# S5 outputs that read the scan's states directly: state tables with chunks innermost, and another order of the stage

## The chip, the cores and the metric

The kernel runs on one core of a Trainium2 chip. A core has a matmul engine (TensorE, "PE" in the profile, with its weight loads as "PEld"), a vector engine (VectorE, "DVE"), an activation engine (ScalarE, "ACT"), GpSimd ("POOL") and a queue for transfers (SyncE, "SP"); they share an on-chip memory of 128 partitions (SBUF) and accumulators that TensorE writes (PSUM). The metric is the device time of one execution in microseconds, as the median of the runs.

## The reference

An input of 256 frames by 2048 features runs through two layers, all in float32. The first layer's mixer, the one that the change touches, is a diagonal state-space layer (S5): 128 groups of 16 features, each with 64 complex states.

```python
u = h @ w_in                                    # 256 x 2048
u_g = u.reshape(bsz, seq, S5_GROUPS, S5_GROUP)  # 128 groups of 16
bu = einsum('blgc,gpc->blgp', u_g, bb)          # complex, 64 states each
s  = associative_scan(s_t = ab * s_(t-1) + bu_t) over the frames
y  = einsum('blgp,gcp->blgc', s_re, c_re) - einsum('blgp,gcp->blgc', s_im, c_im)
z  = gelu(y + d_skip * u)
z  = z * sigmoid(z @ w_glu)
return z @ w_out
```

After it come a squared-ReLU MLP, then a chunked gMLP mixer and a second MLP, with RMS norms around each. These take the most time and the change leaves them as they are.

## The kernel before

The program is written in the order in which it runs: every engine works through its own queue in program order, and no scheduler moves anything. An instruction that waits holds up all that stands behind it on its engine.

**Large products.** A weight is taken in panels. One step of a panel (`kstep`) takes a 128-row slice of a weight, splits it into a high part (ScalarE, L145) and a low part (VectorE, L146), and issues 12 matmuls of 128x512 (L171). The left side is a slab, which `tgroup` fills from transposes (L271) with a high part (L275, ScalarE) and a low part (L276, VectorE). `w_in` alone is multiplied without the split: `win_panel(p, hooks)` runs panel p in 16 steps of two 128x512 matmuls (L183), and after step n calls what stands in `hooks[n]`.

**The S5 stage.** The 256 frames form 64 chunks k of 4 frames j. The 128 groups form two halves h of 64 groups, handled in pairs: 32 rows r per half, with two groups gp = 0, 1 in each row; i = 0, 1 is the real or imaginary part. The states of a group fill 64 partitions.
- `u_tr`, `u_load`: u is transposed and, through DRAM (`ud`), laid out by groups.
- `v_group(h, b)`: for eight rows r, matmuls (L830) give what each chunk adds to the states, in an accumulator; four copies of 64x512 (ScalarE L841, VectorE L839) put it into `s_t`.
- `scan(i)`: a scan over the 64 chunks in five levels up and five down. A level is four VectorE operations (L859 to L862): two products with a table `sc_t` into temporaries, two additions into the states. It handles 31, 15, 7, 3 or 1 chunks of 32 floats each: 992, 480, 224, 96 or 32 elements a partition. Scans 0 and 1 belong to h = 0 (16 rows each), 2 and 3 to h = 1. `scan_some(i, n)` issues the next n levels.
- `y_states(h, b)`: copies the states of eight rows from `s_t` into `sst` (ScalarE L884, VectorE L882), shifted by one chunk, with real and imaginary parts stacked on 128 partitions.
- `y_group(h, b)`: for each of eight rows, two matmuls on 128 partitions (L895: states times the table that `prep_w2` made in `xw`) and two on 64 (L898: u times `t_t`), then eight gelu activations (L904) into `zv`.
- `z_t(h, b)` is `tgroup` of `zv` into the slab for GLU. `idle_fill(n)` issues n matmuls without use (L264).

The trace records a plain float32 matmul as two entries ("passes" below), so a `win_panel` step is L183 x4 in it and a row of y_group L895 x4 and L898 x4.

Accumulators come from a pool of three; panel 2 of `w_in` holds one while v and y groups share the rest, and the GLU panel `pg` later holds two. `s_t` lies with chunks outermost and rows innermost:

```python
    s_t = [g6.rearrange("p (k i r) -> p k i r", i=2, r=32)] + [
        t.rearrange("p (k i r) -> p k i r", i=2, r=16) for t in (g3[:, 0:2048], g0[:, 0:2048])]
```

Loads of weights and `u_load` are issued on the SP queue in program order.

Of the kernel before, what the change touches and what calls it, by code (L numbers as in the profile page):

```python
# [30 lines left out]
def kernel(  # L31
# [672 lines left out]
    def table_mul(dst, tab0, h, st_sw, j, tm):  # L704
# [15 lines left out]
          for s in (g4[:, 0:2048], spare, g5[:, 0:2048], g0[:, 2048:4096])]  # L720
    t_t = [s[:, 2048:4096].rearrange("p (r j c) -> p r j c", j=4, c=16) for s in (g4, g5)]

    s_t = [g6.rearrange("p (k i r) -> p k i r", i=2, r=32)] + [
        t.rearrange("p (k i r) -> p k i r", i=2, r=16) for t in (g3[:, 0:2048], g0[:, 0:2048])]
    ust = [g6[:, 0:2048].rearrange("p (n d) -> p n d", n=2)] + [
        g7[:, 0:1024].rearrange("p (n d) -> p n d", n=2)] * 2
    utp = [g6[:, 2048:4096].rearrange("p (b a t) -> p b a t", b=4, a=2)] + [
        g7[:, 1024:2048].rearrange("p (b a t) -> p b a t", b=2, a=2)] * 2
    sst = [g8[:, i * 1024:(i + 1) * 1024].rearrange("p (r q k) -> p r q k", q=2, k=64)
           for i in range(2)]  # L730

# [4 lines left out]
    def prep_w2(h, j):  # L736
        table_mul(x_t[h], 8 + 2 * j, h, bc_t[h, "c"], j, tmw)

# [82 lines left out]
    def u_zero(q):  # L821
        G.memset(ub[q], 0.0)

    def u_of(h, r):
        return ub[2 * h + r // 16][:, r % 16, :]

    def v_group(h, b):
        ps = accp.tile([128, 1024], F32, tag="acc", name="acc")
        for q in range(8):
            T.matmul(ps[:, q * 128:(q + 1) * 128], lhsT=w1_t[h, b][:, q, :],  # L830
                     rhs=u_of(h, 8 * b + q), start=True, stop=True)
        sv, r0 = sv_of(h, b)
        pv = ps.rearrange("p (r g k) -> p g r k", g=2, k=64)
        for gp in range(2):
            for ri in range(2):
                o = sv[gp * 64:gp * 64 + 64, :, ri, r0:r0 + 8].rearrange("p k r -> p r k")
                i = pv[ri * 64:ri * 64 + 64, gp]
                if gp and h == 0:
                    V.tensor_copy(o, i)  # L839
                else:  # L840
                    S.activation(out=o, in_=i, func=AF.Copy)  # L841

    def sv_of(h, b):
        return (s_t[0], 8 * b) if h == 0 else (s_t[1 + b // 2], 8 * (b % 2))

    def scan(i, tmp):

        h, r0, nr = i // 2, 16 * (i % 2), 16
        s = s_t[0][:, :, :, r0:r0 + 16] if h == 0 else s_t[i - 1]

        def level(lv, k0):
            d, step = 1 << lv, 2 << lv
            n = (62 - k0) // step + 1
            dst = s[:, k0:k0 + (n - 1) * step + 1:step]
            src = s[:, k0 - d:k0 - d + (n - 1) * step + 1:step]
            t = [x[:, 0:n * 2 * nr].rearrange("p (n i r) -> p n i r", i=2, r=nr) for x in tmp]
            a, b = [sc_t[:, lv, k, h, :, r0:r0 + nr].unsqueeze(1).to_broadcast([128, n, 2, nr])
                    for k in (0, 1)]
            V.tensor_tensor(out=t[0], in0=src, in1=a, op=ALU.mult)  # L859
            V.tensor_tensor(out=t[1][:, :, ::-1, :], in0=src, in1=b, op=ALU.mult)  # L860
            V.tensor_tensor(out=dst, in0=dst, in1=t[0], op=ALU.add)
            V.tensor_tensor(out=dst, in0=dst, in1=t[1], op=ALU.add)  # L862
# [10 lines left out]

    def y_states(h, b):
        dst = sst[b % 2]
        sv, r0 = sv_of(h, b)
        for ri in range(2):
            for gp in range(2):
                o = dst[ri * 64:ri * 64 + 64, :, gp, 1:64]
                i = sv[gp * 64:gp * 64 + 64, 0:63, ri, r0:r0 + 8].rearrange("p k r -> p r k")  # L880
                if gp and h:
                    V.tensor_copy(o, i)  # L882
                else:
                    S.activation(out=o, in_=i, func=AF.Copy)  # L884

    def y_group(h, b):
        dst = sst[b % 2]
        w2 = xw[h].rearrange("p (g m) -> p g m", m=64)
        tv = t_t[h].rearrange("p r j c -> p r (j c)")
        ps = accp.tile([128, 1024], F32, tag="acc", name="acc")  # L890
        for q in range(8):
            r = 8 * b + q
            o = [ps[0:64, gp * 512 + q * 64:gp * 512 + q * 64 + 64] for gp in range(2)]
            for gp in range(2):
                T.matmul(o[gp], lhsT=dst[:, q, gp, :], rhs=w2[:, 2 * r + gp, :], start=True,  # L895
                         stop=False)
            for gp in range(2):
                T.matmul(o[gp], lhsT=u_of(h, r)[gp * 64:gp * 64 + 64, gp * 64:gp * 64 + 64],  # L898
                         rhs=tv[gp * 64:gp * 64 + 64, r, :], start=False, stop=True)
        c0 = b * 256  # L900
# [12 lines left out]
    with tc.manual_schedule():  # L913
# [71 lines left out]
        def c(f, *args):  # L985
            return lambda: f(*args)
# [28 lines left out]
        def scan_some(i, n):  # L1015
            for _ in range(n):
                next(scs[i], None)

        def sst_zero():
            for t in sst:  # L1020
                G.memset(t[:, :, :, 0:1], 0.0)

        ps = win_panel(1, {
# [11 lines left out]
        ps = win_panel(2, {  # L1035
            0: [c(u_tr, 1, b) for b in range(2)] + [c(u_load, 2), c(y_states, 0, 0)],
            4: [c(y_states, 0, 1)],
            6: [c(v_group, 1, 0)],
            7: [c(v_group, 1, 1), c(scan_some, 2, 99)],
            8: [c(idle_fill, 7), c(y_group, 0, 0)],  # L1040
            10: [c(y_group, 0, 1), c(y_states, 0, 2)],
            12: [c(y_states, 0, 3)],
        })
        u_out(2, ps, r0[0])
        idle_fill(4)
        for b in range(2):
            u_tr(2, b)
        u_zero(3)
        u_load(3)
        y_group(0, 2)  # L1050
        issue_cast(glu_p[0][0] + 2, True)
        slab_z.append(Slab("g6"))
        z_t(0, 0)
        y_group(0, 3)
        more_raw()
        z_t(0, 1)
        pg = new_acc()
        state["hold"] = False
        run_panel(glu_p[0], slab_z, pg, 0, 1)
        z_t(0, 2)  # L1060
        v_group(1, 2)
        z_t(0, 3)
        run_panel(glu_p[0], slab_z, pg, 1, 2)
        v_group(1, 3)
        y_states(1, 0)
        y_states(1, 1)
        slab_z.append(Slab("g3"))
        run_panel(glu_p[0], slab_z, pg, 2, 3)
        scan_some(3, 99)
        idle_fill(4)  # L1070
        y_group(1, 0)
        run_panel(glu_p[0], slab_z, pg, 3, 5)
        y_group(1, 1)
        z_t(1, 0)
        run_panel(glu_p[0], slab_z, pg, 5, 8)
        z_t(1, 1)
        y_states(1, 2)
        y_states(1, 3)
        idle_fill(4)
        run_panel(glu_p[0], slab_z, pg, 8, 9)  # L1080
        y_group(1, 2)
        run_panel(glu_p[0], slab_z, pg, 9, 10)
# [245 lines left out]
```

## Time and profile before

| | |
|---|---|
| runs | 2737.99, 2736.59, 2735.10 us; median 2736.59 |
| profiled execution | 2737.9 us, its span 2735.9 us |
| granted TensorE clock, mean | 0.994 |
| busy share of the span | PE 98%, PEld 79%, DVE 58%, ACT 46%, POOL 0% |
| chain that ended last, by engine | PE 91%, DVE 3%, ACT 2% |
| chain, by line | L171 84%, L183 2%, L830 1% |
| S5 stage, from the first state matmul to GLU step 10 | about 120 to 285 us of the span |

The share of busy time belongs to the whole span, of which the S5 stage is a small part; within it one has to look at stretches (busy time of each engine between two moments), at the chain of work that ended last in order of time, and at single waits. Times in rows of the trace count from the start of the span.

### The profile page before, as it was taken

The page shows a single profiled execution, that of the slowest core. Times are in us where ns is not written, and L with a number is a line of the kernel's source. Part 1 is how long each engine was busy: PE and PEld are TensorE (multiplying, and loading weights), DVE is VectorE, ACT ScalarE, POOL GpSimd, SP SyncE. Part 2 cuts the span into 40 slices and gives each one's busy share as a digit, 9 for nine tenths or more (in the row PEclk, how much of TensorE's full clock was granted, in tenths as well). Part 3 has the DMA queues.
Part 4 walks back from the last instruction along what each step waited for, and adds up shares of the span by engine and source line. Part 5 has one row for each costly group of instructions (what it writes and reads, how often), then busy time and mean ns, then how long its engine had stood idle before and what let it go on. Part 6 is the DMA issues. An engine that isn't in the chain of part 4 may idle for free.

```text
span 2735.9 us, 30661 instructions
## 1 busy us (share of the span) xinstructions
PE 2680.0 (98%) x12395; PEld 2153.3 (79%) x12395; DVE 1591.8 (58%) x1831; ACT 1258.4 (46%) x1438; POOL 12.8 (0%) x23
## 2 busy tenths in 40 slices
PE   8998999999999999999999999999999999999997
PEld 4556887888888888778887788888878888888885
DVE  6686456545555555575558645555575455555555
ACT  5465545444443444454444544444454444443443
POOL 0100000000000000000000000000000000000000
PEclk9999999999999999999999999999999999999998
DMA  7432475555555555655556555555655555555553
GB/s 188 149 112 93 159 238 169 189 185 191 192 185 193 192 184 186 199 201 187 197 191 209 185 189 193 188 185 198 231 173 183 199 185 187 191 191 187 194 189 108
DMA packets 149629, 502.30 MB, mean 184 GB/s; under 512 B 21856, under 2 KB 30192, under 8 KB 148208
## 3 DMA queue, kind: packets, MB, share of 16 engines
q1 hardware_dynamic: 148896, 500.02, 54.3%
q8 instruction: 97, 1.59, 0.2%
q10 hardware_dynamic: 592, 0.33, 0.0%
q14 instruction: 44, 0.36, 0.0%
HBM read 494.02 MB, written 6.29 MB: 183 GB/s over the span
## 4 chain that ended last, share of the span: by engine, by line
PE 91%; DVE 3%; ACT 2%; issue 1%; DMA 0%; SPq 0%; DVEq 0%; ACTq 0%
PE acc L171 84%; PE acc L183 2%; PE tr L271 2%; PE tr L1241 1%; DVE lo L146 1%; PE acc L830 1%; PE tr L264 0%; ACT g L884 0%; PE acc L895 0%; DVE g L328 0%; PE acc L898 0%; ACT g L841 0%; DVE g L352 0%; DVE g L347 0%; ACT big L904 0%
## 5 line engine op out<-in xcount | busy, mean ns | idle before, releaser
L171 PE MATMUL acc<-hi,sl_g 128*128 128x512 f32 x6912 | 1881.7, 392 | 2.6 <-DVE g L328 1.1
L171 PEld LDWEIGHTS acc<-hi,sl_g 128*128 128x128 f32 x6912 | 1294.3, 188 | 276.9 <-DVE g L328 2.4
L146 DVE TENSOR_TENSOR lo<-raw,hi 128x1024 fp32r<-128x1024 f32 x652 | 797.2, 1225 | 689.4 <-ACT hi L145 682.2
L171 PE MATMUL acc<-lo,sl_g 128*128 128x512 f32 x3456 | 1067.9, 390 | 11.3 <-DVE lo L146 11.3
L145 ACT ACTIVATE hi<-raw 128x1024 fp32r<-128x1024 f32 x652 | 691.0, 1061 | 805.9 <-PE acc L171 805.7
L171 PEld LDWEIGHTS acc<-lo,sl_g 128*128 128x128 f32 x3456 | 649.5, 188 | 147.9 <-DVE lo L146 12.1
L146 DVE TENSOR_TENSOR lo<-spare,hi 128x1024 fp32r<-128x1024 f32 x212 | 259.5, 1225 | 287.1 <-ACT hi L145 287.1
L145 ACT ACTIVATE hi<-spare 128x1024 fp32r<-128x1024 f32 x212 | 224.8, 1062 | 323.7 <-PE acc L171 323.7
L183 PE MATMUL acc<-raw,g 128*128 128x512 f32 x256 | 117.5, 604 | 0.1
L276 DVE TENSOR_TENSOR sl_g<-tr,sl_g 128x512 fp32r<-128x512 f32 x104 | 67.3, 686 | 64.5 <-ACT sl_g L275 64.5
L275 ACT ACTIVATE sl_g<-tr 128x512 fp32r<-128x512 f32 x104 | 57.1, 595 | 86.9 <-PE tr L271 86.5
L183 PEld LDWEIGHTS acc<-raw,g 128*128 128x128 f32 x256 | 47.1, 193 | 50.2 <-issue 49.3
L1148 DVE TENSOR_TENSOR g<-acc,g 128x1024 f32<-128x1024 f32 x48 | 56.4, 1217 | 0.0
L271 PE MATMUL tr<-ident,big 128*128 128x128 f32 x416 | 55.0, 273 | 0.1
L271 PEld LDWEIGHTS tr<-ident,big 128*128 128x128 f32 x416 | 48.3, 141 | 8.3 <-ACT big L1242 1.7
L1127 DVE TENSOR_TENSOR big<-big 128x1024 f32<-128x1024 f32 x32 | 39.2, 1226 | 5.2 <-ACT big L1126 3.0
L1126 ACT ACTIVATE big<-acc,st 128x1024 f32<-128x1024 f32 x32 | 35.8, 1119 | 8.7 <-PE acc L171 8.7
L264 PE MATMUL tr<-ident 128*128 128x512 f32 x68 | 33.2, 625 | 6.6 <-DVE sl_g L314 6.6
L1242 ACT ACTIVATE big<-tr,bsT 128x384 f32<-128x384 f32 x32 | 18.6, 582 | 41.6 <-PE tr L1241 40.6
L904 ACT ACTIVATE big<-acc 32x256 f32<-32x256 f32 x64 | 23.9, 374 | 27.4 <-PE acc L898 26.7
L1234 DVE TENSOR_TENSOR big<-big,g 128x768 f32<-128x768 f32 x32 | 30.7, 958 | 1.1
L841 ACT ACTIVATE g<-acc 64x512 f32<-64x512 f32 x24 | 25.7, 1069 | 11.4 <-PE acc L830 11.1
(172 smaller groups left out, 850.5 us busy)
## 6 DMA issues: line engine op xcount, KB each, us to landing
raw<-in_ffn_w_up_dram SPq DMA_DIRECT2D x96, 1024.0 KB, 5.1
raw<-in_ffn_w_down_dram SPq DMA_DIRECT2D x96, 1024.0 KB, 5.2
raw<-in_sgu_w_in_dram SPq DMA_DIRECT2D x72, 1024.0 KB, 5.1
raw<-in_sgu_w_out_dram SPq DMA_DIRECT2D x36, 1024.0 KB, 5.3
spare<-in_ffn_w_up_dram SPq DMA_DIRECT2D x32, 1024.0 KB, 5.0
spare<-in_ffn_w_down_dram SPq DMA_DIRECT2D x32, 1024.0 KB, 5.3
spare<-in_sgu_w_in_dram SPq DMA_DIRECT2D x24, 1024.0 KB, 5.0
raw<-in_s_w_in_dram SPq DMA_DIRECT2D x15, 1024.0 KB, 6.3
```

What stands on the lines that cost most here:

```text
L145: S.activation(out=hi, in_=src, func=AF.Copy)
L146: V.tensor_tensor(out=lo, in0=src, in1=hi.bitcast(F32), op=ALU.subtract)
L171: T.matmul(half(ps, j), lhsT=l, rhs=r[:, j * 512:(j + 1) * 512], start=first and w == 0, stop=last and w == which[-1])
L183: T.matmul(ps[n][:, j * 512:(j + 1) * 512], lhsT=lhs[n], rhs=raw_t[i][:, k, j * 512:(j + 1) * 512], start=first, stop=last)
L264: T.matmul(ps, lhsT=ident, rhs=ident.unsqueeze(1).to_broadcast([128, 4, 128]), start=True, stop=True)
L271: T.transpose(out=ps[:, a * 256 + n * 128:a * 256 + n * 128 + 128], in_=src(kt + a, n), identity=ident)
L275: S.activation(out=slab.hi[:, o:o + 512], in_=ps, func=AF.Copy)
L276: V.tensor_tensor(out=slab.lo[:, o:o + 512], in0=ps, in1=slab.hi32[:, o:o + 512], op=ALU.subtract)
L1126: S.activation(out=tmp[n], in_=ps[n], func=AF.Relu, scale=rs[:, n:n + 1])
L1127: V.tensor_tensor(out=tmp[n], in0=tmp[n], in1=tmp[n], op=ALU.mult)
L1148: V.tensor_tensor(out=acc[:, n, c], in0=ps[n], in1=acc[:, n, c], op=ALU.add)
L1234: V.tensor_tensor(out=vt[:, :, c], in0=vt[:, :, c], in1=t[h % 2].unsqueeze(1).to_broadcast([128, 2, HD]), op=op)
```

## The change

It lays the states out as `(i r k)`, chunks innermost and shifted by one chunk, so that chunk 0 is zero (`s_zero`, on GpSimd, L854) and y_group reads `s_t` as it stands. The table of `prep_w2` is laid out by real and imaginary part on the 64 partitions of each group (`w2_t`), by four half-sized additions in place of one (L741, L746). `y_states`, `sst` and `sst_zero` go. y_group issues per row two matmuls with u (L896) and four with states (L899), all on 64 partitions, in pairs for the two halves of the rows. v_group writes 64x8x63, contiguous in k (L849 VectorE, now for h = 1; L851 ScalarE). The scan's operations (L872 to L875) step through k, which is innermost. The fillers (7, 4, 4 and 4) go, and the calls from panel 2 on stand in another order: scan 3 goes level by level between GLU steps.

```diff
-    s_t = [g6.rearrange("p (k i r) -> p k i r", i=2, r=32)] + [
-        t.rearrange("p (k i r) -> p k i r", i=2, r=16) for t in (g3[:, 0:2048], g0[:, 0:2048])]
+
+    s_t = [g6.rearrange("p (i r k) -> p i r k", i=2, r=32)] + [
+        t.rearrange("p (i r k) -> p i r k", i=2, r=16) for t in (g3[:, 0:2048], g0[:, 0:2048])]
...
-    sst = [g8[:, i * 1024:(i + 1) * 1024].rearrange("p (r q k) -> p r q k", q=2, k=64)
-           for i in range(2)]
+    w2_t = [s.rearrange("p (r i j c) -> p r i j c", i=2, j=4, c=16) for s in xw]
 
     def prep_w2(h, j):
-        table_mul(x_t[h], 8 + 2 * j, h, bc_t[h, "c"], j, tmw)
+
+        (a, b), (tm1, tm2) = bc_t[h, "c"], tmw
+        gs = slice(64 * h, 64 * h + 64)
+        for o, i, k in ((tm1, a, 0), (tm2, b, 1)):
+            V.tensor_tensor(out=o, in0=i, op=ALU.mult,
+                            in1=tabB[:, 8 + 2 * j + k, gs].unsqueeze(2).to_broadcast([128, 64, 16]))
+        for ri in range(2):
+            for gp in range(2):
+                q = slice(ri * 64, ri * 64 + 64)
+                V.tensor_tensor(out=w2_t[h][gp * 64:gp * 64 + 64, :, ri, j, :],
+                                in0=tm1[q, gp::2, :], in1=tm2[q, gp::2, :], op=ALU.add)
 
...
     def v_group(h, b):
...
         pv = ps.rearrange("p (r g k) -> p g r k", g=2, k=64)
         for gp in range(2):
             for ri in range(2):
-                o = sv[gp * 64:gp * 64 + 64, :, ri, r0:r0 + 8].rearrange("p k r -> p r k")
-                i = pv[ri * 64:ri * 64 + 64, gp]
-                if gp and h == 0:
+                o = sv[gp * 64:gp * 64 + 64, ri, r0:r0 + 8, 1:64]
+                i = pv[ri * 64:ri * 64 + 64, gp, :, 0:63]
+                if gp and h:
                     V.tensor_copy(o, i)
                 else:
                     S.activation(out=o, in_=i, func=AF.Copy)
 
+    def s_zero(i):
+        G.memset(s_t[i][:, :, :, 0:1], 0.0)
+
     def sv_of(h, b):
         return (s_t[0], 8 * b) if h == 0 else (s_t[1 + b // 2], 8 * (b % 2))
 
     def scan(i, tmp):
 
         h, r0, nr = i // 2, 16 * (i % 2), 16
-        s = s_t[0][:, :, :, r0:r0 + 16] if h == 0 else s_t[i - 1]
+        s = s_t[0][:, :, r0:r0 + 16, :] if h == 0 else s_t[i - 1]
 
         def level(lv, k0):
             d, step = 1 << lv, 2 << lv
             n = (62 - k0) // step + 1
-            dst = s[:, k0:k0 + (n - 1) * step + 1:step]
-            src = s[:, k0 - d:k0 - d + (n - 1) * step + 1:step]
-            t = [x[:, 0:n * 2 * nr].rearrange("p (n i r) -> p n i r", i=2, r=nr) for x in tmp]
-            a, b = [sc_t[:, lv, k, h, :, r0:r0 + nr].unsqueeze(1).to_broadcast([128, n, 2, nr])
+            dst = s[:, :, :, k0 + 1:k0 + 1 + (n - 1) * step + 1:step]
+            src = s[:, :, :, k0 + 1 - d:k0 + 1 - d + (n - 1) * step + 1:step]
+            t = [x[:, 0:n * 2 * nr].rearrange("p (i r n) -> p i r n", i=2, r=nr) for x in tmp]
+            a, b = [sc_t[:, lv, k, h, :, r0:r0 + nr].unsqueeze(3).to_broadcast([128, 2, nr, n])
                     for k in (0, 1)]
             V.tensor_tensor(out=t[0], in0=src, in1=a, op=ALU.mult)
-            V.tensor_tensor(out=t[1][:, :, ::-1, :], in0=src, in1=b, op=ALU.mult)
+            V.tensor_tensor(out=t[1][:, ::-1], in0=src, in1=b, op=ALU.mult)
             V.tensor_tensor(out=dst, in0=dst, in1=t[0], op=ALU.add)
             V.tensor_tensor(out=dst, in0=dst, in1=t[1], op=ALU.add)
 
...
-    def y_states(h, b):
-        dst = sst[b % 2]
+    def y_group(h, b):
         sv, r0 = sv_of(h, b)
-        for ri in range(2):
-            for gp in range(2):
-                o = dst[ri * 64:ri * 64 + 64, :, gp, 1:64]
-                i = sv[gp * 64:gp * 64 + 64, 0:63, ri, r0:r0 + 8].rearrange("p k r -> p r k")
-                if gp and h:
-                    V.tensor_copy(o, i)
-                else:
-                    S.activation(out=o, in_=i, func=AF.Copy)
-
-    def y_group(h, b):
-        dst = sst[b % 2]
-        w2 = xw[h].rearrange("p (g m) -> p g m", m=64)
         tv = t_t[h].rearrange("p r j c -> p r (j c)")
         ps = accp.tile([128, 1024], F32, tag="acc", name="acc")
         for q in range(8):
             r = 8 * b + q
             o = [ps[0:64, gp * 512 + q * 64:gp * 512 + q * 64 + 64] for gp in range(2)]
-            for gp in range(2):
-                T.matmul(o[gp], lhsT=dst[:, q, gp, :], rhs=w2[:, 2 * r + gp, :], start=True,
-                         stop=False)
-            for gp in range(2):
-                T.matmul(o[gp], lhsT=u_of(h, r)[gp * 64:gp * 64 + 64, gp * 64:gp * 64 + 64],
-                         rhs=tv[gp * 64:gp * 64 + 64, r, :], start=False, stop=True)
+            half_p = [slice(gp * 64, gp * 64 + 64) for gp in range(2)]
+            for gp, p in enumerate(half_p):
+                T.matmul(o[gp], lhsT=u_of(h, r)[p, p], rhs=tv[p, r, :], start=True, stop=False)
+            for ri in range(2):
+                for gp, p in enumerate(half_p):
+                    T.matmul(o[gp], lhsT=sv[p, ri, r0 + q, :],
+                             rhs=w2_t[h][p, r, ri].rearrange("p j c -> p (j c)"), start=False,
+                             stop=ri == 1)
...
-        def sst_zero():
-            for t in sst:
-                G.memset(t[:, :, :, 0:1], 0.0)
-
         ps = win_panel(1, {
             0: [c(u_tr, 0, 0), c(u_tr, 0, 1), c(u_load, 0), c(u_tr, 0, 2), c(u_tr, 0, 3),
                 c(u_load, 1)],
             4: [c(t_shift, 1)],
-            6: [sst_zero],
+            6: [c(s_zero, 0)],
             7: [c(v_group, 0, 0)],
             8: [c(v_group, 0, 1), c(scan_some, 0, 1)],
             10: [c(v_group, 0, 2), c(scan_some, 0, 2)],
         })
         u_out(1, ps, r0[0])
         ps = win_panel(2, {
-            0: [c(u_tr, 1, b) for b in range(2)] + [c(u_load, 2), c(y_states, 0, 0)],
-            4: [c(y_states, 0, 1)],
+            0: [c(u_tr, 1, b) for b in range(2)] + [c(u_load, 2)],
+            5: [c(s_zero, 1)],
             6: [c(v_group, 1, 0)],
             7: [c(v_group, 1, 1), c(scan_some, 2, 99)],
-            8: [c(idle_fill, 7), c(y_group, 0, 0)],
-            10: [c(y_group, 0, 1), c(y_states, 0, 2)],
-            12: [c(y_states, 0, 3)],
+            9: [c(y_group, 0, 0)],
+            11: [c(y_group, 0, 1)],
         })
         u_out(2, ps, r0[0])
-        idle_fill(4)
+        y_group(0, 2)
         for b in range(2):
             u_tr(2, b)
         u_zero(3)
+        s_zero(2)
         u_load(3)
-        y_group(0, 2)
+        y_group(0, 3)
         issue_cast(glu_p[0][0] + 2, True)
         slab_z.append(Slab("g6"))
         z_t(0, 0)
-        y_group(0, 3)
         more_raw()
         z_t(0, 1)
         pg = new_acc()
         state["hold"] = False
-        run_panel(glu_p[0], slab_z, pg, 0, 1)
+
+        def glu(k0, k1):
+            run_panel(glu_p[0], slab_z, pg, k0, k1)
+
+        glu(0, 1)
+        v_group(1, 2)
         z_t(0, 2)
-        v_group(1, 2)
+        glu(1, 2)
+        v_group(1, 3)
+        scan_some(3, 1)
         z_t(0, 3)
-        run_panel(glu_p[0], slab_z, pg, 1, 2)
-        v_group(1, 3)
-        y_states(1, 0)
-        y_states(1, 1)
+        glu(2, 3)
+        y_group(1, 0)
+        scan_some(3, 1)
+        glu(3, 4)
+        scan_some(3, 2)
+        y_group(1, 1)
+        glu(4, 5)
+        scan_some(3, 3)
         slab_z.append(Slab("g3"))
-        run_panel(glu_p[0], slab_z, pg, 2, 3)
-        scan_some(3, 99)
-        idle_fill(4)
-        y_group(1, 0)
-        run_panel(glu_p[0], slab_z, pg, 3, 5)
-        y_group(1, 1)
+        glu(5, 6)
+        scan_some(3, 1)
+        glu(6, 7)
         z_t(1, 0)
-        run_panel(glu_p[0], slab_z, pg, 5, 8)
+        scan_some(3, 1)
+        glu(7, 8)
         z_t(1, 1)
-        y_states(1, 2)
-        y_states(1, 3)
-        idle_fill(4)
-        run_panel(glu_p[0], slab_z, pg, 8, 9)
+        scan_some(3, 1)
+        glu(8, 10)
         y_group(1, 2)
-        run_panel(glu_p[0], slab_z, pg, 9, 10)
+        glu(10, 11)
         y_group(1, 3)
-        run_panel(glu_p[0], slab_z, pg, 10, 11)
+        glu(11, 12)
         z_t(1, 2)
         z_t(1, 3)
-        run_panel(glu_p[0], slab_z, pg, 11, 16)
+        glu(12, 16)
 
```

Names in the rows below: `g_84` and `g_82`, `g_80` are the states `s_t[0]`, `s_t[1]`, `s_t[2]` (memory g6, g3, g0), `g_85` (g8) holds the scan's temporaries and before also `sst`, `acc` an accumulator, `raw` a loaded weight slice, `hi` and `lo` its parts, `sl_g` a slab's low and high part. Sizes are those of the result.

On VectorE, at the end of scan 1 and the start of scan 2. Before:

```order
L861 TENSOR_TENSOR g_84<-g_84,g_85 128x31x2x16
L862 TENSOR_TENSOR g_84<-g_84,g_85 128x31x2x16
L859 TENSOR_TENSOR g_85<-g_82,sc_t 128x992
L860 TENSOR_TENSOR g_85<-g_82,sc_t 128x31x2x16
L861 TENSOR_TENSOR g_82<-g_82,g_85 128x31x32
```

After:

```order
L874 TENSOR_TENSOR g_84<-g_84,g_85 128x2x16x31
L875 TENSOR_TENSOR g_84<-g_84,g_85 128x2x16x31
L849 COPY g_82<-acc 64x8x63 x4
L872 TENSOR_TENSOR g_85<-g_82,sc_t 128x992
L873 TENSOR_TENSOR g_85<-g_82,sc_t 128x2x496
L874 TENSOR_TENSOR g_82<-g_82,g_85 128x32x31
```

The four copies of v_group(1,0) and v_group(1,1) out of their accumulators now stand here, behind all of scan 1; before, ScalarE made them.

On TensorE, in panel 2 of `w_in`, from v_group(1,0) to the first y_group. Before:

```order
L830 MATMUL acc<-g_81,w_670 128x128 x8
L183 MATMUL acc<-raw_88,g_80 128x512 x2
L830 MATMUL acc<-g_81,w_702 128x128 x8
L183 MATMUL acc<-raw_89,g_80 128x512 x2
L264 MATMUL tr<-ident 128x512 x7
L895 MATMUL acc<-big,g_85 64x64 x2
L898 MATMUL acc<-g_83 64x64 x2
```

After:

```order
L840 MATMUL acc<-g_81,w_682 128x128 x8
L183 MATMUL acc<-raw_88,g_80 128x512 x2
L840 MATMUL acc<-g_81,w_714 128x128 x8
L183 MATMUL acc<-raw_89,g_80 128x512 x4
L896 MATMUL acc<-g_83 64x64 x2
L899 MATMUL acc<-big,g_84 64x64 x4
```

A panel step (two more L183) stands where the fillers stood, and y_group(0,0) reads g_84, the states, in place of g_85, their copy; its accumulator is the one that v_group(1,0) used.

On VectorE, at the end of scan 3 (`g_80`). Before:

```order
L860 TENSOR_TENSOR g_85<-g_80,sc_t 128x31x2x16
L861 TENSOR_TENSOR g_80<-g_80,g_85 128x31x32
L862 TENSOR_TENSOR g_80<-g_80,g_85 128x31x32
L146 TENSOR_TENSOR lo<-raw_87,hi 128x1024
L146 TENSOR_TENSOR lo<-raw_88,hi 128x1024
```

After, its last levels:

```order
L875 TENSOR_TENSOR g_80<-g_80,g_85 128x32x7
L146 TENSOR_TENSOR lo<-raw_89,hi 128x1024
L276 TENSOR_TENSOR sl_g_1721<-tr,sl_g_1721 128x512
L872 TENSOR_TENSOR g_85<-g_80,sc_t 128x480
L873 TENSOR_TENSOR g_85<-g_80,sc_t 128x2x240
L874 TENSOR_TENSOR g_80<-g_80,g_85 128x32x15
L875 TENSOR_TENSOR g_80<-g_80,g_85 128x32x15
L146 TENSOR_TENSOR lo<-raw_89,hi 128x1024
L276 TENSOR_TENSOR sl_g_1721<-tr,sl_g_1721 128x512
```

The ten levels stood in one piece ahead of two low casts of GLU; now low casts and a slab's low parts stand between the levels.

## The prediction

> **What bounds the kernel now.** I read the page first: span, busy times, granted clock, shares of the chain.
>
> ```profile
> span 2735.9 us, 30661 instructions
> PE 2680.0 (98%) x12395; PEld 2153.3 (79%) x12395; DVE 1591.8 (58%) x1831; ACT 1258.4 (46%) x1438; POOL 12.8 (0%) x23
> PEclk9999999999999999999999999999999999999998
> PE 91%; DVE 3%; ACT 2%; issue 1%; DMA 0%; SPq 0%; DVEq 0%; ACTq 0%
> ```
>
> TensorE is the bound nearly everywhere, so only places where it waits, or does work that goes, can pay. The change touches the S5 stage, some 160 us of 2735.9. Next I read that stage by stretches (columns: length, busy time of each engine, clock, DMA): from the first state matmul of y_group(0,0) to the first GLU matmul, and on to the end of GLU step 10, after which nothing of the stage is open.
>
> ```profile
> 168.18:207.47 39.29, 38.50 (x309) 24.42 (x309) 28.40 (x50) 28.51 (x47) 1.80 (x1) 1.00 0.27 82
> 207.47:285.44 77.97, 66.83 (x457) 50.28 (x456) 41.10 (x65) 44.83 (x71) 0.00 (x0) 0.93 0.29 95
> ```
>
> TensorE is busy in both, partly with fillers; the second has 11.1 us idle and a lower clock. The chain in order of time says where fillers and y groups lie; the 5-us windows and one timeline row show the largest hole.
>
> ```profile
> 124.11 1.78 PE acc L830 x16
> 125.90 3.44 PE acc L183 x8
> 143.21 0.87 PE tr L804 x8
> 160.26 1.72 PE acc L183 x4
> 161.98 6.01 PE tr L264 x14
> ...
> 168.85 0.38 PE acc L895 x4
> 169.23 0.26 PE acc L898 x4
> ...
> 197.19 2.34 DMA ud<-big
> ...
> 202.50 2.07 DMA g<-ud
> ...
> 262.44 0.44 PE tr L271 x4
> 262.87 3.44 PE tr L264 x8
> 266.31 2.75 PE acc L171 x12
> ```
> ```profile
> 245.00:250.00 5.00, 0.00 (x0) 0.00 (x0) 4.90 (x7) 1.89 (x3) 0.00 (x0) 0.67 0.00 0
> 250.00:255.00 5.00, 2.71 (x6) 2.15 (x7) 5.00 (x5) 0.00 (x0) 0.00 (x0) 0.50 0.29 84
> ```
> ```profile
> 252.29 0.79 PE L171 MATMUL acc<-lo,sl_g 128*128 128x512 f32 x1 [9.00 <-DVE lo L146]
> ```
>
> L264 is idle_fill. At 252.29 a GLU step waits 9.00 us for its lo cast, which stood on VectorE behind the whole of scan 3, and TensorE resumes at half clock. So the stage is set by VectorE's scans where TensorE waits, and by fillers and y groups elsewhere. The scans (VectorE busy, clock, DMA):
>
> ```profile
> 130.20:154.77 24.57, 23.83 (x45) 1.00 0.46 144
> 154.77:175.12 20.35, 19.70 (x41) 1.00 0.25 87
> 175.12:195.55 20.43, 19.77 (x41) 1.00 0.31 103
> ```
>
> Scan 0 takes 24.57 because two pairs of v_group copies sit in it; scans 1 and 2 show the bare scan, S = 20.35.
>
> **The change, part by part.** Durations by shape, VectorE, then ScalarE (busy and mean ns, then idle before); then two small contiguous copies, and the start of prep_w2(1):
>
> ```profile
> L862 DVE TENSOR_TENSOR g<-g,g 128x992 f32<-128x992 f32 x8 | 9.5, 1192 | 0.3
> L859 DVE TENSOR_TENSOR g<-g,sc_t 128x992 f32<-128x992 f32 x8 | 9.5, 1189 | 0.2
> L839 DVE COPY g<-acc 64x512 f32<-64x512 f32 x8 | 8.3, 1035 | 8.4 <-ACT g L841 8.3
> L276 DVE TENSOR_TENSOR sl_g<-tr,sl_g 128x512 fp32r<-128x512 f32 x8 | 5.4, 688 | 8.0 <-ACT sl_g L275 7.9
> L882 DVE COPY g<-g 64x504 f32<-64x504 f32 x8 | 4.9, 611 | 0.2
> L146 DVE TENSOR_TENSOR lo<-raw,hi 128x1024 fp32r<-128x1024 f32 x16 | 19.3, 1223 | 41.0 <-ACT hi L145 41.0
> ```
> ```profile
> L884 ACT ACTIVATE g<-g 64x504 f32<-64x504 f32 x24 | 25.9, 1081 | 10.5 <-DVE g L862 10.0
> L841 ACT ACTIVATE g<-acc 64x512 f32<-64x512 f32 x24 | 25.7, 1069 | 11.4 <-PE acc L830 11.1
> L904 ACT ACTIVATE big<-acc 32x256 f32<-32x256 f32 x64 | 23.9, 374 | 27.4 <-PE acc L898 26.7
> L145 ACT ACTIVATE hi<-raw 128x1024 fp32r<-128x1024 f32 x16 | 16.7, 1057 | 14.0 <-PE acc L171 13.7
> L275 ACT ACTIVATE sl_g<-tr 128x512 fp32r<-128x512 f32 x8 | 4.7, 596 | 2.2 <-PE tr L271 2.1
> ```
> ```profile
> L585 DVE COPY g<-g x3: 189/189/190, 16.6 to 19.1; 128x64 f32<-128x64 f32 x3
> L1226 DVE COPY st<-st x1: 161/161/161, 1440.5 to 1440.5; 128x2 f32<-128x2 f32 x1
> ```
> ```profile
> 102.33 0.69 DVE L771 TENSOR_TENSOR g<-tr,big 128x512 f32<-128x512 f32 x1 [11.51 <-PE tr L759]
> 103.13 1.23 DVE L710 TENSOR_TENSOR big<-bst,g 128x1024 f32<-128x1024 f32 x1
> ```
>
> *The scans, which no row shows in their new form.* Their four operations per level now step through k with k innermost, by 2, 4, 8, 16 and 32 floats; before, 16 floats lay together. The five levels have 992, 480, 224, 96 and 32 elements, up and down. What a stride costs, by the nearest rows: L882 (reads 128 B apart) takes 0.611 us for 504, where contiguous copies have a slope of (189 − 161)/62 = 0.45 ns an element, so 0.161 + 502 × 0.45 = 0.387: +0.44 ns. L839 (writes 128 B or more apart) 1.035 against 0.69 for 512 of L276, also from PSUM: +0.67. L841 and L884 1.07 and 1.08 against 0.60 of L275: +0.92 and +0.95. The mean is +0.75 ns. The bounds: nothing (20.35), and 0.75 at every level with the in-place additions (L861, L862) paying for read and write one after another: six payments for four operations, 2 × 1824 × 6 × 0.75 = 16.4, so 36.8. I take one payment per operation at the levels from 16 B on: 4 × 2 × 832 × 0.75 = 5.0, S = 25.4; level 0, 8 B apart, stands between adjacent and far and I leave it free.
>
> [...]
>
> *y_group, also without a row.* Before, an r has four 128-row passes (0.38) and four 64-row passes (0.26): 0.64, and 5.1 for eight. One pass of 64 columns streams in about 64/512 of a 0.43-us L183 matmul, 0.054; four plus two (64-row passes in pairs side by side) make 0.33, so half of the 0.64 goes where the rows change size. After: twelve 64-row passes, six pairs, 6 × 0.054 = 0.33 and no change of size, 2.6 for eight, with 0.3 for entering: Y = 2.9. Bounds: 2.6, and three times the 0.26 of the present 64-row four, 6.2. I take 2.9, nearest to what streaming gives.
>
> *Copies.* The 16 y_states copies on ScalarE and VectorE per half (L884, L882) go. v_group's copies are contiguous: 0.60 (ScalarE) and 0.69 (VectorE) instead of 1.07 and 1.04.
>
> *First stretch, to the first y matmul.* v_group(0,1) ends on TensorE at 124.11 + 1.78 = 125.89; four ScalarE copies of 0.60 make scan 0 ready at 128.3 (before 130.20). VectorE must be free: prep_w2(1) has four quarters of 2 × 1.22 + 4 × 0.69 = 5.2, from 103.13 to 123.9, a margin of 4.4. Scans 0 and 1 take 50.8, without copies inside. y_group(0,0) takes the accumulator slot that v_group(1,0) leaves, and this group's two VectorE copies (L849) stand behind scan 1: 1.3 more. So it starts at 128.4 + 50.8 + 1.3 = 180.5 instead of 168.18: **+12.3**. Behind it on TensorE's queue waits everything else: step 9 of panel 2 ends about 163.7 (160.26 + 1.72 + 1.72), and TensorE then stands idle for 17 us.
>
> *Second stretch, to the first GLU matmul (39.3 before).* After: Y 2.9; 2.3 lost to a half clock after the idle time (in the windows above it was 0.50 after 9 us of it; half of the first 4.6 us); two steps 3.4, Y, four steps 6.9, Y, u_tr 1.0, Y; then the last gelu 8 × 0.374 + 0.1 = 3.1, two hi casts 2.1, one L275 0.6. Together 4 × 2.9 + 2.3 + 3.4 + 6.9 + 1.0 + 5.8 = 31.0: **−8.3**, first GLU matmul at 211.5. Four fillers lay in this stretch and go, 3.4; the seven of 161.98 (6.01) lie ahead of it, where TensorE waits anyway. Scan 2 ends about 207, before the lo casts.
>
> *Third stretch (78.0 before).* Two GLU steps 5.5, two v groups 3.6, two sets of transposes (L271) 0.9 and copies 1.5 come ahead of scan 3: 11.5, it starts at 223.0. From there VectorE is the bound: S 25.4, six lo casts 7.3 and three L276 2.1, level by level, to 257.8. y_group(1,2) 2.9, gelu 3.1 (GLU step 10, 2.75, beside it), y_group(1,3) 2.9: 266.7. 55.2 instead of 78.0: **−22.8**, of which 9.0 is the wait at 252.29, 7 the two fillers (L264, 3.44 each), the rest y_states and shorter y groups.
>
> *Costed at nothing:* prep_w2(0), +5.2 us, lies in the 11.51 us that VectorE waits before L771; the s_zero memsets are on GpSimd, idle there. u_load(3) on the SP queue comes after u_tr(2), which now stands behind y_group(0,2); from the store to the last load it takes 7.4 us (197.19 to 204.57), so from about 206 to 213.4, and v_group(1,2) needs it at 214.2: covered by 0.8, and what it is late beyond that adds to the third stretch. If a cover is gone, prep_w2(1) delays all by its excess over 4.4.
>
> Sum: 12.3 − 8.3 − 22.8 = −18.8. The profiled execution took 2737.9 us (span 2735.9), 1.3 above the median of 2736.59; so 2719.1 by it and **2718 on the median**. A longer S counts three times (two scans in the first stretch, one in the third), a longer Y six times: gain = 18.8 − 3 (S − 25.4) − 6 (Y − 2.9).
>
> **Rivals.**
> 1. *Strides are free.* S = 20.4: gain 33.8, 2703. For it: VectorE's other inputs here are broadcast tables, L859 runs no slower than L862. Against it: L882 and L839. [...]
> 2. *8 bytes already pay.* 2 × 4 × 992 × 0.75 = 6.0 more, S = 31.4: gain 0.8, 2736, no change. For it: nothing here is 8 bytes apart and large.
> 3. *64-row pairs don't run side by side.* Y 5.1 to 6.2: gain 5.6 to −1.0, 2731 to 2738. For it: 0.26 for four passes is more than 0.22 for four streamed singly.
> 4. *The other side: in-place additions pay twice at all levels.* S = 36.8: loss 15.4, 2752. It decides from S = 31.7, where the gain is used up: then TensorE waits for scans 0 and 1 beyond 190 us and later work doesn't give it back. For it: L839, writes, is dearer than L882, reads. Against it: a read and a write of one element in one pass should overlap.
>
> **How the numbers follow.** Forecast 0.48 (its own range 2711 to 2726: S ± 2, Y ± 0.3). Rival 1: 0.12; rival 2: 0.13; rival 3: 0.12; rival 4: 0.10; others 0.05. The range reaches from 2700 to 2740: it holds all but rival 4 and half of the others. 0.2%, 5.5 us, is about what a measurement of this kernel tells from no change. Faster, below 2731: forecast, rival 1, half of rival 3 and a little of the others, 0.68; same: most of rival 2 and half of rival 3, 0.16; slower, above 2742: rival 4, the upper edge of 2, and others, 0.16.
>
> **What would show it.** Right: scan 1 in a window of 24 to 27 us, with the 480-element form at about 1.0 instead of 0.66 and the 992 one at 1.19; y_group(0,0) near 180 after 17 us idle; a y group of 2.9 us; first GLU matmul near 211; no wait of 9 us for a lo cast; GLU step 10 over by 267. Wrong: a 992-element form above 1.5 us, y groups of 5 us, a bound other than VectorE between 223 and 258, or a hole that I didn't see behind prep_w2(1) or the loads.

## The result

The changed kernel takes 2724.06 us (median of four runs, 2721.54 to 2726.18) against 2737.27 of the kernel before on the same chip: a ratio of 0.9946, 95% interval 0.9934 to 0.9958, so 13.2 us less where 18.8 were forecast. The profiled execution took 2724.23, its span is 2722.4 against 2735.9. The page of the kernel after, the lines that answer to those shown of before:

```profile
span 2722.4 us, 31091 instructions
PE 2653.4 (97%) x12613; PEld 2141.8 (79%) x12613; DVE 1615.6 (59%) x1847; ACT 1220.3 (45%) x1414; POOL 13.0 (0%) x24
PEclk9988999999999999999999999999999999999998
```

VectorE has 24 us more to do, ScalarE 38 less, and two slices of the S5 stage now show a lower clock. The stage by stretches, cut at the same pieces of work as before (the wait ahead of y_group(0,0), then to the first GLU matmul, then until GLU step 10 and y_group(1,3) are both over; before, step 10 came last of the two, now y_group(1,3) does):

```profile
168.18:180.26 12.08, 0.00 (x0) 0.03 (x1) 11.83 (x15) 0.00 (x0) 0.00 (x0) 0.50 0.00 0
180.26:211.92 31.66, 26.75 (x424) 19.69 (x425) 27.67 (x44) 16.92 (x42) 1.90 (x2) 0.88 0.26 87
211.92:270.76 58.84, 53.91 (x564) 43.95 (x564) 44.73 (x62) 25.25 (x44) 0.00 (x0) 0.91 0.41 134
```

Before, y_group(0,0) starts at 168.18 and the other two stretches take 39.29 and 77.97: 12.1 lost, 7.6 and 19.1 gained, together 14.7 at the end of the third. The scans, VectorE's operations and TensorE's waits between 100 and 300 us (us in total, times, longest):

```profile
128.09:153.46 25.37, 24.71 (x40) 1.00 0.42 126
153.46:178.74 25.28, 24.59 (x42) 0.78 0.23 82
```
```profile
L875 DVE TENSOR_TENSOR g<-g,g 128x992 f32<-128x992 f32 x8 | 9.6, 1194 | 0.3
L874 DVE TENSOR_TENSOR g<-g,g 128x480 f32<-128x480 f32 x8 | 8.4, 1044 | 0.0
L872 DVE TENSOR_TENSOR g<-g,sc_t 128x480 f32<-128x480 f32 x8 | 8.2, 1030 | 0.2
```
```profile
PE acc L896 <- DVE g L849: 16.9, 1, 16.9
PE acc L171 <- ACT sl_g L275: 6.0, 2, 4.9
PE acc L171 <- DVE lo L146: 3.1, 3, 2.5
PE acc L899 <- DVE g L875: 1.3, 1, 1.3
```

A scan takes 25.37 instead of 20.35, the longest wait is the 16.9 us of y_group(0,0) for VectorE's copies (L849) behind scan 1, and the longest wait for a low cast is 2.5 instead of 9.0. The chain that ended last shows a y group's rows: u passes and state passes follow one another without a gap, 0.35 us a row, 2.8 for eight. From a group's first pass to the work behind it, it is 2.9 (188.93 to 191.87).

```profile
268.15 0.23 PE acc L899 x8
268.38 0.12 PE acc L896 x4
```

The first GLU matmul, and the first and the last operation of scan 3 in that chain:

```profile
211.92 1.22 PE L171 MATMUL acc<-hi,sl_g 128*128 128x512 f32 x2 [4.91 <-ACT sl_g L275]
```
```profile
226.40 1.19 DVE g L872
259.08 1.21 DVE g L875
```

### The profile page after: what moved, and what is told of

Its sections match the earlier page's. It is cut to its first block, busy times and chain, and to the rows that moved or that the text cites. A ratio compares the mean times of both kernels' runs of the same rounds, so it can differ in the third digit from the quotient of the medians.

```text
span 2722.4 us, 31091 instructions
## 1 busy us (share of the span) xinstructions
PE 2653.4 (97%) x12613; PEld 2141.8 (79%) x12613; DVE 1615.6 (59%) x1847; ACT 1220.3 (45%) x1414; POOL 13.0 (0%) x24
## 4 chain that ended last, share of the span: by engine, by line
PE 88%; DVE 3%; ACT 1%; issue 0%; DVEq 0%; ACTq 0%
PE acc L171 84%; PE tr L271 2%; PE tr L1245 1%; DVE lo L146 0%; PE tr L264 0%; DVE g L328 0%; ACT hi L145 0%; ACT big L906 0%; DVE g L352 0%; DVE g L347 0%; DVE g L872 0%; DVE g L874 0%; DVE g L873 0%; PE acc L899 0%; ACT big L336 0%
## 5 line engine op out<-in xcount | busy, mean ns | idle before, releaser
L183 PE MATMUL acc<-raw,g 128*128 128x512 f32 x256 | 117.6, 604 | 0.1
L276 DVE TENSOR_TENSOR sl_g<-tr,sl_g 128x512 fp32r<-128x512 f32 x104 | 67.2, 686 | 56.6 <-ACT sl_g L275 56.5
L275 ACT ACTIVATE sl_g<-tr 128x512 fp32r<-128x512 f32 x104 | 57.0, 595 | 89.6 <-PE tr L271 89.2
L183 PEld LDWEIGHTS acc<-raw,g 128*128 128x128 f32 x256 | 47.1, 193 | 50.2 <-issue 49.4
L872 DVE TENSOR_TENSOR g<-g,sc_t 128x992 f32<-128x992 f32 (+4 forms) x40 | 26.4, 661 | 5.5 <-ACT g L851 4.4
L875 DVE TENSOR_TENSOR g<-g,g 128x992 f32<-128x992 f32 (+4 forms) x40 | 26.8, 671 | 1.4
```

Of the source, the lines that this page charges most:

```text
L183: T.matmul(ps[n][:, j * 512:(j + 1) * 512], lhsT=lhs[n], rhs=raw_t[i][:, k, j * 512:(j + 1) * 512], start=first, stop=last)
L275: S.activation(out=slab.hi[:, o:o + 512], in_=ps, func=AF.Copy)
L276: V.tensor_tensor(out=slab.lo[:, o:o + 512], in0=ps, in1=slab.hi32[:, o:o + 512], op=ALU.subtract)
```

## The experiments

All are edits of the changed kernel unless the text says otherwise; each ratio is against the kernel before on the same chip. The traces are shifted against one another: scan 0 starts between 127.88 and 130.35 us in the changed kernel and its variants. So a difference of up to 2.5 us between times of two single traces says nothing, unless both are counted from the start of scan 0.

**The accumulator wait.** The copies of v_group(1,0) and (1,1) go to ScalarE.

```diff
-                if gp and h:
+                if gp and h and b >= 2:
```

> The four accumulator copies of v_group(1,0) and (1,1) go to ScalarE; the rest is the changed kernel (2724.06, y_group(0,0) at 180.26 after 16.87 us idle, first GLU matmul at 211.92). Theory A (the accumulator slot is the wait, VectorE's queue the bound behind it): y_group(0,0) starts at 163.5, right after step 9; scan 2 starts 2.8 earlier and ends at 204; the two low casts and the slab's low parts stand behind it, so the first GLU step waits there and is over near 210 instead of 216.7; 6 to 7 us less in all, 2717.5. Rival B (the scan's states, not the slot, hold y_group(0,0)): it stays near 177.5, only the 2.8 of VectorE copies go, 2721. Rival C (TensorE is the bound from there on): all 16.8 are gained, 2707.

Measured 2719.62 us, ratio 0.9926 (0.9910 to 0.9943). The start of y_group(0,0), then TensorE's waits with their releasers:

```profile
165.09 0.33 PE L896 MATMUL acc<-g 64*64 64x64 f32 x4
```
```profile
194.66 1.22 PE L171 MATMUL acc<-hi,sl_g 128*128 128x512 f32 x2 [4.91 <-ACT sl_g L275]
207.43 1.22 PE L171 MATMUL acc<-lo,sl_g 128*128 128x512 f32 x2 [11.55 <-DVE lo L146]
```

The wait of 16.9 us is gone (y_group(0,0) follows step 9 at 165.1), so the slot was its cause. 11.55 us of it come back at the first low cast, which stands behind scan 2. The gain is a few microseconds, as theory A had it: the panel of GLU ends 4.0 earlier as the traces stand, 6.1 counted from the start of scan 0 (130.15 here, 128.09 in the changed kernel). The median is 4.4 lower; the intervals of the two ratios overlap.

**The stride.** Levels 1 to 4 of the scans work on neighbouring states.

```diff
+            if lv:
+                dst, src = s[:, :, :, 32:32 + n], s[:, :, :, 0:n]
```

> The scan's levels 1 to 4 read and write as many states as before, but neighbouring ones instead of ones 16 to 128 bytes apart (so the states are other numbers; order and counts are those of the changed kernel). Theory A (the stride costs 5 us a scan, and a scan counts three times): the 480-element operations fall from 1.03 to 0.66 us, S from 25.3 to 20.4, y_group(0,0) from 180.3 to 170.3, the end of y_group(1,3) by 15: 2709. Rival B (TensorE or ScalarE becomes the bound in the third stretch): only the two scans ahead of y_group(0,0) count, 10 us, 2714. Rival C (the operations are slower for the broadcast table with k innermost, not for the stride): S stays at 25, 2724.

Measured 2709.05 us, ratio 0.9889 (0.9874 to 0.9903). VectorE's groups and the wait ahead of y_group(0,0):

```profile
L876 DVE TENSOR_TENSOR g<-g,g 128x480 f32<-128x480 f32 x8 | 5.2, 650 | 0.0
L874 DVE TENSOR_TENSOR g<-g,sc_t 128x480 f32<-128x480 f32 x8 | 5.2, 653 | 0.2
```
```profile
168.92 0.48 PE L898 MATMUL acc<-g 64*64 64x64 f32 x4 [5.72 <-DVE g L849]
```

The tables are broadcast as before, only the addresses differ, and the 0.38 us are gone: the stride is the price. A scan takes 19.7, 5.7 less; y_group(0,0) starts 11.3 earlier, y_group(1,3) ends at 254.3 instead of 270.8, 16.4 earlier. Three times 5.7 is 17.1: a scan does count three times.

**Pairs of halves.** Per row, three matmuls of one half, then three of the other.

```diff
             for gp, p in enumerate(half_p):
                 T.matmul(o[gp], lhsT=u_of(h, r)[p, p], rhs=tv[p, r, :], start=True, stop=False)
-            for ri in range(2):
-                for gp, p in enumerate(half_p):
+                for ri in range(2):
                     T.matmul(o[gp], lhsT=sv[p, ri, r0 + q, :],
...
```

> y_group issues, for each row, the three matmuls of one partition half and then the three of the other, instead of pairs of the two halves; the same matmuls and sums. Theory A (a y group fell from 5.1 to 2.8 us because neighbours on two halves run side by side): twelve passes one after another, 12 x 0.054 = 0.65 us a row, Y = 5.2, six of them count: 14 us more, 2738. Rival B (it fell because no 128-row pass stands between 64-row passes any more, and pairs don't matter): Y stays at 2.8, 2724.

Measured 2725.60 us, ratio 0.9948 (0.9933 to 0.9963): no change, rival B's number, but not its reason. The passes of TensorE in y_group(1,3):

```profile
270.79 0.22 PE L898 MATMUL acc<-big,g 64*64 64x64 f32 x1
270.79 0.22 PE L896 MATMUL acc<-g,g 64*64 64x64 f32 x1
270.85 0.22 PE L898 MATMUL acc<-big,g 64*64 64x64 f32 x1
270.85 0.22 PE L896 MATMUL acc<-g,g 64*64 64x64 f32 x1
```

A state pass of one half and a u pass of the other still start at the same moment. So the kernel that follows separates the halves by 48 passes.

```diff
+        for gp in range(2):
+            p = slice(gp * 64, gp * 64 + 64)
+            for q in range(8):
+                r = 8 * b + q
+                o = ps[0:64, gp * 512 + q * 64:gp * 512 + q * 64 + 64]
+                T.matmul(o, lhsT=u_of(h, r)[p, p], rhs=tv[p, r, :], start=True, stop=False)
+                for ri in range(2):
+                    T.matmul(o, lhsT=sv[p, ri, r0 + q, :],
...
```

> y_group issues the 24 matmuls of the lower partition half for all eight rows, then the 24 of the upper half. Theory A (the two halves run at the same time as separate streams, and a few matmuls of queue were enough to keep both busy when they came three by three): 48 passes in a row on one half leave the other idle, Y = 48 x 0.055 x 2 = 5.3 instead of 2.8, six of them: 10 to 14 us more than 2724, 2734 to 2738. Rival B (only the missing change between 128 and 64 rows made y groups shorter): Y stays at 2.8, 2724.

Measured 2753.87 us, ratio 1.0057 (1.0040 to 1.0074). y_group(0,0), the steps behind it and y_group(0,1), with the clock in the third column from the end:

```profile
181.91:192.00 10.09, 10.09 (x97) 9.97 (x97) 9.90 (x11) 0.00 (x0) 0.00 (x0) 0.50 0.01 2
192.00:197.20 5.20, 5.20 (x9) 2.02 (x8) 4.92 (x19) 2.98 (x8) 0.00 (x0) 0.68 0.01 2
197.20:202.70 5.50, 5.50 (x97) 5.49 (x96) 5.36 (x9) 0.00 (x0) 0.00 (x0) 1.00 0.59 194
```

At full clock a y group now takes 5.5 instead of 2.9, 0.69 a row instead of 0.35: the halves do run as two streams, and their overlap saves nearly half of a y group's time. The cost in all, 30 us, is more than six times 2.6: two of the groups run at half clock (10.09 instead of 5.04 at the first), and the two panel steps behind the first take 5.2 instead of 3.6. The rest of the 30 was not taken apart.

**Fillers.** In the changed kernel, matmuls without use ahead of y_group(0,0) and of the first GLU transposes.

```diff
-            9: [c(y_group, 0, 0)],
+            9: [c(idle_fill, 19), c(y_group, 0, 0)],
...
+        idle_fill(4)
         z_t(0, 0)
```

> Matmuls without use fill the waits of TensorE ahead of y_group(0,0) (19 of them, about 16.3 us of the 16.9) and ahead of the first GLU transposes (4, 3.4 us of the 4.9). Theory A (after an idle stretch the clock is at about half for some 5 us, and this cost 2.1 us in y_group(0,0) and 2.0 in the first GLU step): y_group(0,0) takes 2.9 instead of 5.04, the first GLU step 2.8 instead of 4.75; the first of the two is partly given back in the wait for ScalarE and VectorE ahead of GLU: 2 to 4 us less, 2720 to 2722. Rival B (the slow first y_group is the start of its data, not the clock): y_group(0,0) still 5 us, 2724 or later.

Measured 2722.95 us, ratio 0.9943 (0.9928 to 0.9957): by the time it can't be told from the changed kernel. In the trace y_group(0,0) takes 3.0 us, from 181.24 to 184.25, at full clock, against 5.04 without the fillers, and the first GLU step 3.8 instead of 4.8; the span is 2.0 shorter. The clock of the changed kernel in y_group(0,0), in the first GLU step and at y_group(1,2):

```profile
180.26:185.30 5.04, 5.04 (x97) 4.97 (x97) 4.96 (x6) 0.00 (x0) 0.00 (x0) 0.54 0.01 3
211.90:216.70 4.80, 4.74 (x12) 3.41 (x13) 2.08 (x3) 0.46 (x2) 0.00 (x0) 0.61 0.66 147
260.00:265.00 5.00, 4.58 (x94) 4.50 (x95) 2.54 (x3) 0.30 (x1) 0.00 (x0) 0.66 0.76 261
```

And the kernel before without its nineteen fillers in the stage:

```diff
-            8: [c(idle_fill, 7), c(y_group, 0, 0)],
+            8: [c(y_group, 0, 0)],
...
-        idle_fill(4)
...
-        idle_fill(4)
...
-        idle_fill(4)
```

> The kernel before without its fillers (19 matmuls in the S5 stage), nothing else. Theory A (they only covered waits for the state copies, which stay): the same time within 0.2%, or up to 3 us more by the lower clock after the idle time: 2737 to 2742. Rival B (10 us of them lie on the path, as the forecast's credits of 3.4 and 7 had it): 2728 to 2731.

Measured 2751.37 us, ratio 1.0047 (1.0032 to 1.0062), 14 us slower: both theories fell. Where fillers stood, waits appear that they had covered; and in two stretches the clock is down for long:

```profile
172.03 0.66 PE L895 MATMUL acc<-big,g 128*64 128x64 f32 x4 [5.72 <-issue]
203.00 0.33 PE L804 MATMUL tr<-ident,big 128*128 128x128 f32 x1 [3.90 <-ACT big L797]
243.54 0.45 PE L895 MATMUL acc<-big,g 128*64 128x64 f32 x4 [3.81 <-ACT g L884]
```
```profile
172.00:190.00 18.00, 17.97 (x134) 12.11 (x134) 17.47 (x33) 8.49 (x13) 0.00 (x0) 0.70 0.00 1
204.00:228.00 24.00, 24.00 (x155) 18.67 (x154) 3.75 (x4) 10.49 (x24) 0.00 (x0) 0.52 0.30 89
```

After a wait of 5.72 us ahead of y_group(0,0), TensorE is busy for 18 us at a mean clock of 0.70; after the wait of 3.90 it is 0.52 from 204 to 228. The kernel before shows 1.00 in both stretches.

**The interleaving of scan 3.** Scan 3 in one piece where its first level stood (the first `scan_some(3, 1)` becomes `scan_some(3, 99)`, the others go).

> The changed kernel with scan 3 in one piece where its first level stood, ahead of the low casts of the GLU steps, as in the kernel before. Theory A (the interleaving is what took away the wait of 9.0 us): scan 3 ends near 252 instead of 260, but a GLU step waits some 17 to 20 us for its low cast behind it, and ten steps follow after it instead of six: 7 to 10 us more than 2724, 2731 to 2734. Rival B (only the end of scan 3 counts): 2716.

Measured 2736.49 us, ratio 0.9995 (0.9986 to 1.0005): the whole gain is gone.

```profile
254.21 1.22 PE L171 MATMUL acc<-lo,sl_g 128*128 128x512 f32 x2 [16.91 <-DVE lo L146]
```

The wait of 9.0 us of the kernel before is back, at 16.9: TensorE reaches it at 237.3 instead of 243.3 and goes on at 254.21 instead of 252.29; the scan ends 1.2 later than in the kernel before (252.3 against 251.1).

**Versions meant to be faster.** The first spread scan 2 as well and had all copies of v_group on ScalarE, like the versions after it.

> A version meant to be faster: all copies of v_group on ScalarE, two levels of scan 2 ahead of the first low casts and the other eight between GLU steps, then scan 3; first casts ahead of y_group(0,3), whose gelus come after the first slab part. Theory A (VectorE's queue order holds TensorE): y_group(0,0) near 164, first GLU matmul near 190, no wait over 5 us before scan 3's end; scan 3 ends 9 to 12 earlier than 260: 2712 to 2715. Rival B (u_load(3) or ScalarE takes the place, since both now come 20 us earlier): 2718 to 2722, no better than moving the copies alone (2719.6).

Measured 2729.89 us, ratio 0.9967 (0.9955 to 0.9979), worse than the changed kernel. TensorE's waits, then VectorE at the start of scan 3:

```profile
198.68 3.75 PE L840 MATMUL acc<-g,w 128*128 128x128 f32 x16 [4.78 <-DMA g<-ud]
223.11 0.69 PE L896 MATMUL acc<-big,g 64*64 64x64 f32 x8 [8.91 <-DVE g L872]
```
```profile
232.19 1.23 DVE L146 TENSOR_TENSOR lo<-raw,hi 128x1024 fp32r<-128x1024 f32 x1 [9.14 <-ACT hi L145]
```

u_load(3) is late by 4.8, y_group(1,0) waits 8.9 for scan 2 (a later y group waits 8.8 for scan 3), and between them VectorE, the bound, stands 9.1 us idle: scan 3's first level is queued behind a low cast whose high part waits for TensorE. So the next one keeps scan 2 whole and brings v_group(1,2), (1,3) and y_group(1,0) forward.

```diff
+        v_group(1, 2)
+        v_group(1, 3)
+        y_group(1, 0)
         glu(0, 1)
+        scan_some(3, 1)
         z_t(0, 2)
         glu(1, 2)
```

> All copies of v_group on ScalarE and scan 2 in one piece, as in the first variant (2719.6, where TensorE waited 11.6 us for low casts behind scan 2), and v_group(1,2), v_group(1,3) and y_group(1,0) put into that wait, so that scan 3 can follow scan 2 at once, level by level between low casts that wait for nothing. Theory A (VectorE's queue is the bound from 128 us on, and any idle time in it shows in the end): scan 2 ends at 204, scan 3 starts near 210 instead of 226 and ends near 247 instead of 260: 13 us less than 2724, 2710 to 2712. Rival B (u_load(3) or the half clock after idle time gives it back): 2716 to 2720.

Measured 2713.45 us, ratio 0.9905 (0.9889 to 0.9922); and the same kernel again, beside the last one below:

> The same kernel as e8_v_first, on the same chip as the one it is compared with: 2712 to 2715 is expected by either theory.

2711.57 us, ratio 0.9899 (0.9884 to 0.9914). In the trace of the first of the two, scan 3 starts at 215.9 and ends at 251.2, 9 us earlier than in the changed kernel, 11 counted from the start of scan 0 (130.07); it starts later than expected since VectorE waits ahead of it:

```profile
214.78 1.23 DVE L146 TENSOR_TENSOR lo<-raw,hi 128x1024 fp32r<-128x1024 f32 x1 [5.09 <-ACT hi L145]
```

With ten fillers in the wait for u_load(3) (7.9 us there):

> The same with ten matmuls without use (8.6 us) ahead of the first GLU transposes, where TensorE waits for u_load(3). Theory A (the clock costs nothing where VectorE is the bound): within 2 us of the kernel without them. Rival B (the half clock after that wait is on the path): 3 to 6 us less than without them.

2715.53 us, ratio 0.9913 (0.9898 to 0.9928): nothing gained, as theory A had it. And with scan 3's first level ahead of that low cast:

> The previous best (2713.5) with the first level of scan 3 ahead of the third low cast on VectorE's queue instead of behind it; there VectorE waited 5.1 us for the high part of that cast. Theory A (idle time of VectorE before scan 3's end shows one to one): scan 3 starts near 211 and ends near 246 instead of 251: 5 us less, 2708.5. Rival B (TensorE and ScalarE now set the casts, so the wait only moves to a later one): 2712 to 2714.

2711.08 us, ratio 0.9900 (0.9879 to 0.9922), beside 2711.57 without it: not to be told apart by time. Scan 3's first operation starts 8.0 us after the last level of scan 2 began instead of 13.0 (the two rows of each, this kernel first); the scan's end gains 2.3 of these 5, the rest is waited for at later casts.

```profile
201.92 1.19 DVE L869 TENSOR_TENSOR g<-g,sc_t 128x992 f32<-128x992 f32 x1
209.93 1.18 DVE L869 TENSOR_TENSOR g<-g,sc_t 128x992 f32<-128x992 f32 x1
```
```profile
199.42 1.19 DVE L869 TENSOR_TENSOR g<-g,sc_t 128x992 f32<-128x992 f32 x1
212.43 1.19 DVE L869 TENSOR_TENSOR g<-g,sc_t 128x992 f32<-128x992 f32 x1
```

## Why the prediction was right, and where it was off

- **Scans: right.** S = 25.4 was forecast and is 25.37; the 992-element operations, 8 bytes apart, take 1.19 as before, the 480-element ones 1.03 to 1.04. The addition in place costs the same as the multiplication (1.19 and 1.19, 1.04 and 1.03), so rival 4 is out; 5 us of stride put rival 1 out, and the free 8 bytes rival 2. The price of 0.75 ns was the mean of two rows of VectorE (0.44 and 0.67) and two of ScalarE (0.92 and 0.95), both of VectorE too low; that it lies so near the measured 0.79 (1.03 against 0.65 us for 480 elements 16 bytes apart) is in part luck. That 8 bytes apart would be free was a choice of the author's that no row of before shows; the 1.19 us of the 992-element operations bear it out. With a time that follows from the element count alone the 480-element operation would have stayed at 0.66; the measured 1.03 decides against it for this stride.
- **First stretch: right.** y_group(0,0) starts at 180.26 (forecast 180.5) after 16.9 us; the copies behind scan 1 are the reason, shown by the kernel that moves them.
- **y groups: right.** 2.9 at full clock (2.9). Rival 3 is out: two streams side by side, shown by the kernel that separates them (5.5). That half of the time of a row before, 0.64 us, went into changes between 128 and 64 rows was the author's estimate; 0.35 a row fits it, but it wasn't tried by itself.
- **Second stretch:** 31.66 (31.0), 0.7 longer than forecast; no single piece stands out.
- **Third stretch: the term that was mis-sized.** 58.84 where 55.2 was forecast, 3.6 longer. Scan 3 starts 14.5 us after the first GLU matmul, not 11.5: after 4.9 us of waiting the first GLU step runs at a clock of 0.61 and takes 4.8 instead of 2.75, and copies wait for it. The scan with its casts took 33.9 us of the 34.8 forecast. At the other end y_group(1,2) runs mostly at half clock (0.51 from 260.3 to 263.5), 4.2 instead of 2.9, after two short waits of 2.5 and 1.3. The sum has the half clock once, behind the longest wait, and it comes three times. In the kernel with fillers the first GLU step takes 3.8 and y_group(1,2) 2.8, both at full clock, and the stretch is 56.5 (211.63 to 268.10): that is 2.4 of the 3.6. There the clock is down earlier, beside the same two waits (2.5 and 1.1): its mean is 0.66 from 255 to 260 and 1.00 from 260 on, for y_group(1,2); what sets the moment was not settled.
- **Behind the third stretch:** the sum had nothing there. The L275 of y_group(1,3) comes after its gelus with too little beside them (a wait of 1.1), and the end of the panel is 12.7 ahead of before (292.73 against 305.38) where the third stretch ended 14.7 ahead; the rest of these 2.0 was not laid out. The span ends 13.5 ahead; the 0.9 gained behind the panel is not explained.
- **Fillers: a wrong credit.** "7 the two fillers", and 3.4 of another, were booked as gains. Taking the fillers out of the kernel before makes it 14 us slower: they covered waits for the state copies, and with them the clock was 1.00 in the two stretches that show 0.70 and 0.52 without them. What the fillers had covered went with the copies; and without the interleaving nothing is gained: with scan 3 in one piece the time is 2736.5. Whether the old layout with the new order would have gained as much was not tried, so no run divides the gain between layout and order. The sum was 5.6 too high and no worse since the stretches were laid out by what waits for what, not by adding up credits.
- **The formula** (gain falls by three for each us of S, by six for each of a y group): three holds (17.1 expected, 16.4 in the trace, 15.0 in time); six did not: at 2.6 us more the cost was 30, not 16. No run tried a small change of a y group.

## What to carry to other kernels

Between two orders of a stage, first find the engine whose queue sets the end (here VectorE, in a kernel where TensorE is 98% busy) and read where it stands idle or what stands behind its long pieces: moving v_group's copies off VectorE and bringing v groups forward, so that it nearly runs through, was worth some 11 us together (the copies alone 4), nearly as much as the whole change. A wait that is removed shows its worth only once the next wait on the same queue is named: 16.9 us gone were 4 to 6 gained. Laying data out for one reader was paid by the other here: 5 us a scan (25.37 against 20.35) for strides of 16 bytes and more, 15 us in all (2724.06 against 2709.05 without the strides), and the kernel gained in spite of it.

## What the runs showed of the hardware that was not expected

- Matmuls on the two 64-row halves overlap even when six passes of one half stand in the queue ahead of the other's six (0.35 us a row either way); with 48 passes of each in a row they no longer do (0.69).
- The clock can stay down while TensorE is busy all the time: after a wait of 5.7 us in the kernel before without its fillers the next 18 us, full of work, had a mean of 0.70, and after a later wait of 3.9 the 24 us from 204 on had 0.52. After 16.9 us of waiting in the changed kernel it was back within about 5 us, with pairs of 64-row passes; with the halves separated it stayed at 0.50 for all 10.09 us of y_group(0,0). What makes the difference was not settled. The length of the wait doesn't order these cases, and rows that alternate between 128 and 64 partitions, as in the first, are not needed for it: the separated halves have none.
- On VectorE strides of 16 and of 32 bytes cost the same: 480 elements +0.38 us, 224 +0.18, that is +0.8 ns an element; an addition with a strided read and a strided write costs hardly more than a multiplication with a strided read alone (1.04 against 1.03 us).
